# A decoder layer on one core: the input x also loaded transposed, small inputs joined, squares, angles and one score step moved

## The chip, the cores and the metric

The kernel runs on one core of a Trainium2 chip. The metric is the device time of one execution in microseconds (us). TensorE is called PE here, and its weight loads, which overlap the matmuls, PEld; VectorE is DVE, ScalarE is ACT, GpSimd is POOL, and SyncE, which issues most transfers, is SP. Each engine takes its own instructions strictly in the order of its queue, so that an instruction that waits holds up all behind it on that engine.

## What is computed

One layer over 256 tokens of 2048 channels: a root-mean-square norm, one wide projection, a recurrent branch and an attention branch with 32 query and 4 key heads, a gated merge, a second norm and an MLP. What matters here is the beginning:

```python
h = rmsnorm(x, norm_mix_pre[l])
proj = h @ w_in[l]
xr, yr, q, k, v, g_rnn, g_attn = jnp.split(proj, IN_OFFSETS, axis=-1)
...
q = rope(q.reshape(B, S, N_Q_HEADS, HEAD_DIM), positions)
k = rope(k.reshape(B, S, N_KV_HEADS, HEAD_DIM), positions)
```

The division by the norm is not applied to x before the projections. They run on x times the gain, and 1/rms of each token is multiplied in later, so the squares of x are needed only when the first results are used.

## The kernel before

**Two parts for each number.** Every matmul of the projections runs in a 32-bit format of reduced precision. Each operand is therefore split into a rounded high part and the rest, the low part, and a product is three matmuls: high by high, low by high, high by low. `Stream` does this for the weights. It loads them in halves of 128x1024 numbers (512 KB, tile `wraw`), ACT casts a half to the high part (`whi`, line 94), and DVE subtracts to get the low part (`wlo`, line 95). The halves 0 to 9 have buffers of their own; those behind share four (`WRAW`), so that the load of half j+4 waits for DVE's `wlo` of half j. The split parts have six buffers (`WHALF`), so that the cast of half j+6 waits until PE is through with half j. The splits run six halves ahead of PE (`AHEAD`).

**x.** PE needs x with channels on the partitions. Before, x arrives with tokens on the partitions, in two row blocks of four quarters (256 KB each, lines 336 and 339), PE transposes it in 32 blocks against an identity (`turn`, line 375, tile `ptr` in PSUM), ACT multiplies each block by the gain and casts it to the high part of `hT` (`part`, line 382), and DVE makes the low part (line 385). Both engines read PSUM there.

**The first projection.** `kv_step(j)`, for j from 0 to 7, multiplies two of the sixteen 128-channel blocks of x by half j of the key and value weights: 12 matmuls of 512 columns, into two banks `kv0` and `kv1` (line 396). Order in the code: the transposes of one quarter, its `part`, a split, a step, the next quarter's transposes. `pin` (keep_in_program_order) holds these instructions in the order in which the code is written; elsewhere a scheduler orders the instructions of each engine. In the last quarter `squares` sums the squares of x, four on ACT (line 405) and four on DVE (line 403).

**What follows.** For each of four groups of heads one pass over 8 halves for the gate (`g`) and one for the queries (`q`): 96 matmuls each (lines 294 to 298). Side work is written as generators in a list `waiting`; `pump()` runs the next piece, and is called after each half. The first is `keys_values`: it takes the norms (`first_norm`, with the square root on ACT), spreads 1/rms over the partitions with two small matmuls (`pr`, line 448, read from `spread`), scales the values, turns the keys by their angles (`rope`), and transposes them (`pk`, line 526). `attention(g)` follows; in it `scores` makes the products `sc` (line 560, pinned), and `masked` takes them out of PSUM on DVE (line 572). In the last group the third score step has to reuse the banks of the second, so that it waits for `masked` of the second.

The angles (position by frequency, reduced modulo two pi by nine small DVE instructions, then two sines on ACT) come behind the first projection, unpinned. Positions, frequencies, sinks and per-channel vectors are four small transfers on SP's queue, behind the first fourteen halves (lines 452 to 458).

Of the kernel before, what the change touches and what calls it, by code (L numbers as in the profile page):

```python
# [25 lines left out]
P = 128  # L26
# [27 lines left out]
class Stream:  # L54
# [3 lines left out]
    def __init__(self, nc, pool, chunks, room, sums):  # L58
        self.nc, self.pool, self.chunks, self.room, self.sums = nc, pool, chunks, room, sums
        self.raw, self.parts = {}, {}  # L60
        self.loaded = self.split = 0
        self.pin = lambda i: i
        self.high = []
        self.at = 0

# [101 lines left out]
def layer(tc, x, g_pre, pos_t, pos_row, inv_freq, vecs, sinks, gains, w_kv, w_q, w_xy, w_rg, w_g, w_rp, w_ap, w_out,  # L167
# [46 lines left out]
    def flat(t):  # L214
        return t.rearrange("p a b c -> p (a b c)")
# [111 lines left out]
    x_nat = [flat(unit(f"x{tb}", F32)) for tb in range(TB)]  # L327
# [4 lines left out]
    gcol = const.tile([P, KT], F32, name="gcol")  # L332
    nc.scalar.dma_start(gcol, g_pre)

    for q in range(4):
        nc.sync.dma_start(x_nat[0][:, quarter(q)], x_v[0][:, quarter(q)])
        if q == 0:
            ws.load_to(1)
        last = nc.sync.dma_start(x_nat[1][:, quarter(q)], x_v[1][:, quarter(q)])
        with tc.issue_after(last.ins):  # L340
            ws.load_to(2 * q + 2)
# [5 lines left out]
    st = const.tile([P, 32], F32, name="st")  # L347
    sq = const.tile([P, 4, TB, 4], F32, name="sqs")
# [20 lines left out]
    ps_t = {}  # L369

    def turn(tb, q):
        ps = ps_t[tb, q] = bank(psm, "ptr")
        for i in range(4):
            k = 4 * q + i
            pin(nc.tensor.transpose(ps[:, i * P : i * P + P], x_nat[tb][:, k * P : k * P + P], ident))

    def part(tb, q, ks=range(4)):
        t = slice(tb * P, tb * P + P)
        ps = ps_t[tb, q]
        for i in ks:  # L380
            g = gcol[:, 4 * q + i : 4 * q + i + 1]
            pin(nc.scalar.activation(hT[q][:, i, 0, t], ps[:, i * P : i * P + P], AF.Copy, scale=g))
        for i in ks:
            g = gcol[:, 4 * q + i : 4 * q + i + 1]
            pin(nc.vector.scalar_tensor_tensor(hT[q][:, i, 1, t], ps[:, i * P : i * P + P], g,
                                               hT[q][:, i, 0, t].bitcast(F32), ALU.mult, ALU.subtract))
# [3 lines left out]
    def kv_step(j):  # L390
        hi, lo = ws.half(False)
        for x, w in ((0, hi), (1, hi), (0, lo)):
            for tb in range(TB):
                for i in range(2):
                    kt = 2 * j + i
                    pin(mm(kv[tb], hT[kt // 4][:, kt % 4, x, tb * P : tb * P + P], w[:, quarter(i)],
                           start=kt == 0 and w is hi and x == 0, stop=kt == KT - 1 and w is lo))

    def squares(tb):
        for q in range(4):  # L400
            x, into = x_nat[tb][:, quarter(q)], sq[:, 0, tb, q : q + 1]
            if tb:
                pin(nc.vector.scalar_tensor_tensor(t2("j"), x, 1.0, x, ALU.mult, ALU.mult, accum_out=into))
            else:
                pin(nc.scalar.activation(t2("j"), x, AF.Square, accum_out=into))

    turn(0, 0)
    turn(1, 0)
    part(0, 0, (0, 1))
    ws.split_high()  # L410
    part(1, 0, (0, 1))
    ws.split_low()
    for tb in range(TB):
        part(tb, 0, (2, 3))
    ws.split_to(2)
    for q in range(4):
        kv_step(2 * q)
        if q < 3:
            turn(0, q + 1)
            turn(1, q + 1)  # L420
            part(0, q + 1)
            part(1, q + 1)
            ws.split_to(2 * q + 4)
        else:
# [9 lines left out]
    def first_norm():  # L434

        pr = bank(psm, "pr")
        spread = t2("spread")
        for tb in range(TB):
# [7 lines left out]
            dg = spread[:, tb * P : tb * P + P]  # L446
            nc.vector.tensor_scalar(dg, ident, r, None, ALU.mult)
            mm(pr[:, tb * P : tb * P + P], ones, dg, start=True, stop=True)
        nc.scalar.copy(rT, pr[:, 0:S])

    pos_i = pa.tile([P, TB], I32, name="pos_i")
    nc.sync.dma_start(pos_i, pos_t)
    ifr = pa.tile([P, 32], F32, name="ifr")
    nc.sync.dma_start(ifr, inv_freq.partition_broadcast(P))
    sink = pa.tile([P, NH], F32, name="sink")
    nc.sync.dma_start(sink, sinks.partition_broadcast(P))
    vec = pa.tile([P, 8, KT], F32, name="vec")
    nc.sync.dma_start(vec, vecs.rearrange("p (a b) -> p a b", a=8))

# [11 lines left out]
    def small(name, shape, dt=F32):  # L471
        return pa.tile(shape, dt, name=name)

    posf = small("posf", [P, TB])
    pin(nc.vector.tensor_copy(posf, pos_i))
    ang = small("ang", [P, TB, 32])
    for tb in range(TB):
        nc.vector.tensor_scalar(ang[:, tb, :], ifr, posf[:, tb : tb + 1], None, ALU.mult)
    turns = small("turns", [P, TB, 32])
    nc.vector.tensor_scalar(turns, ang, 1.0 / TWO_PI, None, ALU.mult)  # L480
    nc.vector.tensor_scalar(turns, turns, 12582912.0, 12582912.0, ALU.add, ALU.subtract)
    for part in two_pi_parts():
        nc.vector.scalar_tensor_tensor(ang, turns, -part, ang, ALU.mult, ALU.add)
    nc.vector.tensor_scalar(ang, ang, 3.1415925, -3.1415925, ALU.min, ALU.max)
    sn = turns
    nc.scalar.activation(sn, ang, AF.Sin)
    cc = small("cc", [P, TB, 2, 32])
    ss = small("ss", [P, TB, 2, 32])
    hs = small("hs", [P, TB, 32])
    nc.scalar.activation(hs, ang, AF.Sin, scale=0.5)  # L490
    nc.vector.tensor_tensor(hs, hs, hs, ALU.mult)
    for i in range(2):
        nc.vector.tensor_scalar(cc[:, :, i, :], hs, -2.0, 1.0, ALU.mult, ALU.add)
        nc.vector.tensor_scalar(ss[:, :, i, :], sn, 1.0 - 2.0 * i, None, ALU.mult)
# [20 lines left out]
    def keys_values(banks):  # L515
        yield
        first_norm()
        for tb in range(TB):
# [3 lines left out]
            rope(banks[tb][:, 0:256], tb, NKV, [k4[:, :, 0, :], k4[:, :, 1, :]])  # L522
            yield
            ps = bank(psm, "pk")
# [3 lines left out]
            yield  # L528

    yatt = []  # L530

    def attention(g, banks):
# [100 lines left out]
        masked(*two)  # L633
        if last_group:
            three = scores(1, 1, [bank(psb, "sc") for par in range(2)])
        yield
# [637 lines left out]
def lay_out(inp):  # L1274
# [26 lines left out]
    def down(w):  # L1301
# [6 lines left out]
    pos = np.asarray(inp["positions"]).reshape(TB, P)  # L1308
    return {
        "x": np.asarray(inp["x"]).reshape(S, D),  # L1310
        "g_pre": per_channel(g("norm_mix_pre")),
        "pos_t": pos.T,
        "pos_row": pos.reshape(S),
        "inv_freq": (10000.0 ** (-np.arange(0, HD, 2, dtype=np.float64) / HD)).astype(np.float32),
# [29 lines left out]
```

## Time and profile before

| What | Value |
|---|---|
| Median of three runs | 1512.02 us (1510.14, 1512.02, 1512.23) |
| The profiled execution | 1509.99 us |
| Its span, first to last instruction | 1508.2 us |
| PE busy | 1492.7 us (99%) |
| DVE busy | 1101.7 us (73%) |
| ACT busy | 828.7 us (55%) |
| Read from HBM | 288.60 MB, 196 GB/s over the span |
| First matmul of `kv_step` | 8.22 us after the span's start |
| First load of the gate pass `g` | 34.19 us |
| First load of the query pass `q` | 58.98 us |

How to read it: the span leaves out what lies before the first and behind the last instruction (1.8 us here). A row of the timeline gives start, duration, engine, line and operation, and in brackets the idle time before it with what ended it. A row of the waits gives the waiting engine, what it waited for, the total in us, the number of times and the longest. A row of the stages gives the stage, its length, the busy time of each engine with the number of instructions, the granted PE clock, and the share and rate of the transfers.

### The profile page before, as it was taken

What the parts mean: (1) busy time and instruction counts of PE and PEld (TensorE: products, weight loads), DVE (VectorE), ACT (ScalarE), POOL (GpSimd) and SP (SyncE); (2) the same over time, 40 slices, a digit from 0 to 9 for tenths busy, and PEclk for the clock granted to TensorE, in tenths of its full rate; (3) what the DMA queues carried; (4) which work ended last, traced back from release to release, by engine and by line L of the source; (5) the groups of instructions that cost most, each with busy time, mean ns of one, the idle gap of its engine ahead of it and who ended that gap; (6) DMA issues with size and microseconds to landing.
All of it is one profiled execution on the core that took longest, in us unless ns stands there. A gap on an engine that the chain in (4) does not pass through costs nothing.

```text
span 1508.2 us, 20012 instructions
## 1 busy us (share of the span) xinstructions
PE 1492.7 (99%) x7600; PEld 1261.5 (84%) x7600; DVE 1101.7 (73%) x1379; ACT 828.7 (55%) x1143; POOL 1.7 (0%) x9
## 2 busy tenths in 40 slices
PE   9999999999999999999999999999999999999997
PEld 7887787889888888888888888888888888888885
DVE  6675677858669966555667866698886666788897
ACT  6554665647566766443355655565454555555453
POOL 0000000000000000000000000000000000000000
PEclk9999999999999999999999999999999999999999
DMA  6645454465646566556764755566667565576665
GB/s 254 221 157 173 148 166 136 157 201 165 213 155 221 170 209 197 192 184 195 268 221 136 270 188 188 194 194 213 217 201 237 195 195 183 193 236 202 204 221 186
DMA packets 83327, 296.19 MB, mean 196 GB/s; under 512 B 9760, under 2 KB 10016, under 8 KB 82208
## 3 DMA queue, kind: packets, MB, share of 16 engines
q1 hardware_dynamic: 79920, 287.58, 57.6%
q10 hardware_dynamic: 3312, 7.35, 1.3%
q8 instruction: 59, 0.97, 0.3%
q14 instruction: 36, 0.29, 0.1%
HBM read 288.60 MB, written 6.29 MB: 196 GB/s over the span
## 4 chain that ended last, share of the span: by engine, by line
PE 84%; DVE 8%; DMA 4%; ACT 2%; issue 1%; DVEq 0%; SPq 0%; ACTq 0%
PE ps L256 21%; PE ps L254 11%; PE dQ L1111 5%; PE pp L298 4%; PE pp L294 4%; PE pp L296 4%; PE g L294 4%; DMA wraw<-in_w_dn 4%; PE g L298 4%; PE g L296 4%; DVE wlo L95 3%; PE s L1111 3%; PE dP L1111 2%; PE q L294 2%; PE q L298 2%; PE q L296 2%
## 5 line engine op out<-in xcount | busy, mean ns | idle before, releaser
L95 DVE TENSOR_TENSOR wlo<-wraw,whi 128x1024 fp32r<-128x1024 f32 x523 | 632.7, 1221 | 306.1 <-ACT whi L94 302.9
L94 ACT CAST whi<-wraw 128x1024 fp32r<-128x1024 f32 x523 | 544.2, 1052 | 554.0 <-PE ps L256 127.3
L256 PE MATMUL ps<-h2T,whi 128*128 128x512 f32 x960 | 223.9, 390 | 0.0
L256 PEld LDWEIGHTS ps<-h2T,whi 128*128 128x128 f32 x960 | 178.3, 188 | 35.6
L256 PE MATMUL ps<-hT,whi 128*128 128x512 f32 x512 | 121.3, 392 | 0.0
L254 PEld LDWEIGHTS ps<-h2T,wlo 128*128 128x128 f32 x960 | 119.1, 192 | 2.3
L254 PE MATMUL ps<-h2T,wlo 128*128 128x256 f32 x960 | 119.9, 283 | 0.0
L256 PEld LDWEIGHTS ps<-hT,whi 128*128 128x128 f32 x512 | 94.7, 188 | 19.8 <-issue 1.1
L1111 PE MATMUL dQ<-whi,uT 128*128 128x512 f32 x288 | 106.9, 389 | 0.0
L294 PE MATMUL g<-whi,hT 128*128 128x512 f32 x256 | 101.3, 396 | 0.0
L296 PE MATMUL g<-wlo,hT 128*128 128x512 f32 x256 | 100.1, 391 | 0.1
L298 PE MATMUL g<-whi,hT 128*128 128x512 f32 x256 | 99.9, 390 | 0.0
L254 PEld LDWEIGHTS ps<-hT,wlo 128*128 128x128 f32 x512 | 63.7, 192 | 1.8 <-issue 0.7
L254 PE MATMUL ps<-hT,wlo 128*128 128x256 f32 x512 | 64.7, 284 | 0.0
L1111 PEld LDWEIGHTS dQ<-whi,uT 128*128 128x128 f32 x288 | 54.1, 188 | 11.2
L294 PEld LDWEIGHTS g<-whi,hT 128*128 128x128 f32 x256 | 48.1, 188 | 10.5 <-issue 1.0
L296 PEld LDWEIGHTS g<-wlo,hT 128*128 128x128 f32 x256 | 48.1, 188 | 10.1 <-DVE wlo L95 0.5
L298 PEld LDWEIGHTS g<-whi,hT 128*128 128x128 f32 x256 | 48.1, 188 | 10.1
L1111 PE MATMUL dQ<-wlo,uT 128*128 128x512 f32 x144 | 56.1, 389 | 0.0
L1111 PE MATMUL dCs<-whi,uT 128*128 128x512 f32 x144 | 54.1, 389 | 0.0
L1111 PE MATMUL dP<-whi,uT 128*128 128x512 f32 x144 | 54.1, 389 | 0.0
L130 DVE TENSOR_TENSOR tlo<-t,thi 128x1536 fp32r<-128x1536 f32 x28 | 49.2, 1757 | 5.1 <-ACT thi L129 5.1
(285 smaller groups left out, 2461.6 us busy)
## 6 DMA issues: line engine op xcount, KB each, us to landing
wraw<-in_w_up SPq DMA_DIRECT2D x128, 512.0 KB, 3.9
wraw<-in_w_dn SPq DMA_DIRECT2D x128, 512.0 KB, 4.5
wraw<-in_w_g SPq DMA_DIRECT2D x64, 512.0 KB, 4.7
wraw<-in_w_xy SPq DMA_DIRECT2D x64, 512.0 KB, 3.7
wraw<-in_w_q SPq DMA_DIRECT2D x32, 512.0 KB, 4.3
wraw<-in_w_ap SPq DMA_DIRECT2D x32, 512.0 KB, 4.8
wraw<-in_w_rp SPq DMA_DIRECT2D x32, 512.0 KB, 4.6
wraw<-in_w_out SPq DMA_DIRECT2D x32, 512.0 KB, 4.9
```

Source lines behind the costliest of these rows:

```text
L94: self.pin(self.nc.scalar.copy(hi, src))
L95: self.pin(self.nc.vector.tensor_tensor(lo, src, hi.bitcast(F32), ALU.subtract))
L130: v.tensor_tensor(lo, t, hi.bitcast(F32), ALU.subtract)
L254: mm(ps[:, f, 1, :], w, a[:, 0, :], start=False, stop=j == 1 and k == 7)
L256: mm(ps[:, f].rearrange("p a b -> p (a b)"), w, a.rearrange("p a b -> p (a b)"), start=kt == 0, stop=j == 3 and k == 7)
L294: mm(banks[tb][n], a[:, 0, t], hi[:, n * 512 : n * 512 + 512], start=first, stop=False)
L296: mm(banks[tb][n], a[:, 0, t], lo[:, n * 512 : n * 512 + 512], start=False, stop=False)
L298: mm(banks[tb][n], a[:, 1, t], hi[:, n * 512 : n * 512 + 512], start=False, stop=last)
L1111: mm(b, a[x], w[y], start=not begun and i == 0, stop=tail and i == 2)
```

## The change

**x comes twice.** The host lays x out a second time with channels on the partitions (`x_t`). Four transfers of 512 KB, the first cut in two, bring it, interleaved with the weight halves, which now come first. `part(k)` takes a whole 128x256 block from SBUF, once on ACT and once on DVE: 16 instructions each where 32 stood. The transposes `turn` are gone. x in its old layout is still loaded for the squares, in eight quarters, behind weight half 11.

**The first half** is split in two pieces of 512 columns (`split_first`), with a `part` between each cast and its subtraction, and step 0 runs one block of channels after the other.

**Small inputs.** Gain, frequencies, sinks, eight vectors and positions come in one transfer of 128x210 numbers (`few`, 105 KB) on ACT's queue at the start. ACT loads its function table before the first data are there (a copy of `eps`).

**Moved.** The angles are a generator of which a piece runs after each of steps 4 to 7, the sines stand behind step 7, pinned before the rest; all eight squares are on ACT and two pieces of `keys_values`; the two matmuls `pr` come last in `keys_values`. In the last group of `attention` the third score step is written one piece later.

```diff
+    def split_first(self, between):
+        src = self.raw.pop(0)
...
+        for i in range(2):
+            c = slice(i * 512, i * 512 + 512)
+            self.pin(self.nc.scalar.copy(hi[:, c], src[:, c]))
+            between(i)
+            self.pin(self.nc.vector.tensor_tensor(lo[:, c], src[:, c], hi[:, c].bitcast(F32), ALU.subtract))
...
-    for q in range(4):
-        nc.sync.dma_start(x_nat[0][:, quarter(q)], x_v[0][:, quarter(q)])
-        if q == 0:
-            ws.load_to(1)
-        last = nc.sync.dma_start(x_nat[1][:, quarter(q)], x_v[1][:, quarter(q)])
-        with tc.issue_after(last.ins):
-            ws.load_to(2 * q + 2)
+    tiny = const.tile([P, 210], F32, name="tiny")
+    nc.scalar.dma_start(tiny, few)
...
+    ws.load_to(1)
+    load_xt(0, 2)
+    load_xt(2, 4)
+    ws.load_to(2)
+    for q in range(1, 4):
+        load_xt(4 * q, 4 * q + 4)
+        ws.load_to(2 * q + 2)
+    ws.load_to(12)
+    x_nat = [[t2("xq") for q in range(4)] for tb in range(TB)]
+    for tb in range(TB):
+        for q in range(4):
+            nc.sync.dma_start(x_nat[tb][q], x_v[tb][:, quarter(q)])
     ws.load_to(2 * EXTRA + WRAW)
...
+    nc.scalar.activation(st[:, 30:31], eps, AF.Copy)
...
+    def part(k):
+        q, i, g, src = k // 4, k % 4, gcol[:, k : k + 1], xt(k)
+        pin(nc.scalar.activation(hT[q][:, i, 0, :], src, AF.Copy, scale=g))
+        pin(nc.vector.scalar_tensor_tensor(hT[q][:, i, 1, :], src, g, hT[q][:, i, 0, :].bitcast(F32), ALU.mult,
+                                           ALU.subtract))
...
-    for q in range(4):
-        kv_step(2 * q)
-        if q < 3:
-            turn(0, q + 1)
-            turn(1, q + 1)
-            part(0, q + 1)
-            part(1, q + 1)
-            ws.split_to(2 * q + 4)
-        else:
-            ws.pin = lambda i: i
-            squares(0)
-            squares(1)
-            ws.split_to(2 * q + 4)
-        kv_step(2 * q + 1)
+    ws.split_first(part)
+    kv_step(0)
+    angle = angles()
+    for j in range(1, 8):
+        for i in range(2):
+            part(2 * j + i)
+        ws.split_high()
+        ws.split_low()
+        kv_step(j)
+        if j > 3:
+            next(angle, None)
+    sines()
+    ws.pin = lambda i: i
     ws.ahead(ws.at - 1)
...
     def keys_values(banks):
         yield
-        first_norm()
+        squares(0)
+        yield
+        squares(1)
+        yield
+        spread = first_norm()
...
+        spread_r0(spread)
...
         masked(*two)
+        yield
         if last_group:
             three = scores(1, 1, [bank(psb, "sc") for par in range(2)])
-        yield
+            yield
         masked(*three)
```

**How the order moves, first place: PE between step 0 and step 2 of the first projection.** `kv0` and `kv1` are the two result banks, `whi1` and `wlo1` the split parts of weight half 1, `ptr` the transposes. Before:

```order
L396 MATMUL kv1_138<-wlo0_159,hT0_133 128x512 x2
L375 MATMUL ptr_185<-ident_111,x0_76 128x128 x4
L375 MATMUL ptr_190<-ident_111,x1_77 128x128 x4
L396 MATMUL kv0_137<-whi1_169,hT0_133 128x512 x2
L396 MATMUL kv1_138<-whi1_169,hT0_133 128x512 x2
L396 MATMUL kv0_137<-wlo1_170,hT0_133 128x512 x2
L396 MATMUL kv1_138<-wlo1_170,hT0_133 128x512 x2
```

Now:

```order
L415 MATMUL kv1_152<-wlo0_160,hT0_147 128x512
L415 MATMUL kv0_151<-whi1_185,hT0_147 128x512 x2
L415 MATMUL kv1_152<-whi1_185,hT0_147 128x512 x2
L415 MATMUL kv0_151<-wlo1_187,hT0_147 128x512 x2
L415 MATMUL kv1_152<-wlo1_187,hT0_147 128x512 x2
L415 MATMUL kv0_151<-whi2_205,hT1_148 128x512 x2
```

The block of eight transposes between the steps is gone, here and at two more places, and the eight ahead of step 0.

**Second place: ACT behind the cast of weight half 10**, which belongs to the gate pass. `xq` are the quarters of x, `turns` and `hs` the two sines, `v_sb` the scaled values. Before:

```order
L94 CAST whi10_395<-wraw10_103 128x1024
L94 CAST whi11_399<-wraw11_105 128x1024
L94 CAST whi12_403<-wraw12_107 128x1024
L94 CAST whi13_460<-wraw13_109 128x1024
L94 CAST whi14_478<-wraw14_407 128x1024
L358 ACT_TABLE_LOAD
L358 ACTIVATE st_114<-st_114,eps_112 128x1 x2
```

Now:

```order
L107 CAST whi10_349<-wraw10_100 128x1024
L421 ACTIVATE xq_104,sqs_129<-xq_104 128x512
L421 ACTIVATE xq_105,sqs_129<-xq_105 128x512
L421 ACTIVATE xq_106,sqs_129<-xq_106 128x512
L107 CAST whi11_353<-wraw11_102 128x1024
L421 ACTIVATE xq_107,sqs_129<-xq_107 128x512
L421 ACTIVATE xq_108,sqs_129<-xq_108 128x512
L450 ACT_TABLE_LOAD
L450 ACTIVATE turns_155<-ang_154 128x64
L451 ACTIVATE hs_158<-ang_154 128x64
L107 CAST whi12_357<-wraw12_120 128x1024
L421 ACTIVATE xq_109,sqs_129<-xq_109 128x512
```

Two more squares, the cast of half 13 and the table load for the square root follow. So all eight squares, a table load and the two sines now stand between the casts of the halves 10 and 13, which stood side by side. On DVE the product of `hs` now stands ahead of `wlo11`.

**Third place: PE at the third score step of the last group**, in the first product of the recurrent branch (`ps`); `sc` are the scores. Before:

```order
L254 MATMUL ps_2332<-hT2_135,wlo77_2166 128x256 x4
L254 MATMUL ps_2332<-hT3_136,wlo77_2166 128x256 x2
L560 MATMUL sc_2359<-kT_457,qT3_2187 128x256
L254 MATMUL ps_2332<-hT3_136,wlo77_2166 128x256
L560 MATMUL sc_2360<-kT_457,qT3_2187 128x256
L254 MATMUL ps_2332<-hT0_133,wlo78_2205 128x256 x4
```

Now:

```order
L267 MATMUL ps_2260<-hT2_149,wlo77_2094 128x256 x4
L267 MATMUL ps_2260<-hT3_150,wlo77_2094 128x256 x2
L579 MATMUL sc_2302<-kT_377,qT3_2115 128x256
L267 MATMUL ps_2260<-hT3_150,wlo77_2094 128x256
L579 MATMUL sc_2303<-kT_377,qT3_2115 128x256
L267 MATMUL ps_2260<-hT0_147,wlo78_2133 128x256 x4
```

The scheduler puts the third score step at the same place among the matmuls as before, although the code has it one piece later.

More of the change, by code (lines that the diff above doesn't have):

```diff
@@ L391, in kv_step @@
         hi, lo = ws.half(False)
[L392 to L397, printed above, removed]
+        for ks in ((0,), (1,)) if j == 0 else ((0, 1),):
+            for x, w in ((0, hi), (1, hi), (0, lo)):
+                for tb in range(TB):
+                    for i in ks:
+                        kt = 2 * j + i
+                        pin(mm(kv[tb], hT[kt // 4][:, kt % 4, x, tb * P : tb * P + P], w[:, quarter(i)],
+                               start=kt == 0 and w is hi and x == 0, stop=kt == KT - 1 and w is lo))
```

136 lines of the change are left out of this document (62 added, 74 removed).

## The prediction

> **What bounds the kernel now.** First the page: its span, its busy times and the chain of work that ended last.
>
> ```profile
> span 1508.2 us, 20012 instructions
> PE 1492.7 (99%) x7600; PEld 1261.5 (84%) x7600; DVE 1101.7 (73%) x1379; ACT 828.7 (55%) x1143; POOL 1.7 (0%) x9
> PE 84%; DVE 8%; DMA 4%; ACT 2%; issue 1%; DVEq 0%; SPq 0%; ACTq 0%
> ```
>
> PE sets the end: 99% busy, 84% of the chain. So the change is worth what it takes out of PE's queue: matmuls that vanish, waits that vanish, and an earlier first matmul; busy time saved on ACT and DVE counts only where PE waited for it. Next the stages of the beginning: up to the first load of the gate pass, that pass, and the first query pass.
>
> ```profile
> 0.00:34.19 34.19, 31.77 (x148) 25.60 (x149) 20.94 (x51) 22.17 (x52) 1.70 (x9) 1.00 0.75 280
> 34.19:58.98 24.79, 23.91 (x110) 19.08 (x109) 21.82 (x55) 17.32 (x23) 0.00 (x0) 1.00 0.60 210
> 58.98:80.75 21.77, 21.77 (x98) 18.04 (x97) 9.80 (x9) 10.03 (x11) 0.00 (x0) 1.00 0.59 192
> ```
>
> The query pass shows the floor: 96 matmuls in 21.77 us, 0.2268 us each, and nothing else. The gate pass has the same 96 and takes 24.79 us. The first projection has 96 too, and ends only at 34.19. Where the difference lies, PE's first row there, the chain and PE's waits tell:
>
> ```profile
> 8.22 2.13 PE L396 MATMUL kv<-whi,hT 128*128 128x512 f32 x8
> ```
>
> ```profile
> 1.64 5.82 DMA x<-in_x
> 11.85 0.87 PE ptr L375 x8
> 18.53 0.87 PE ptr L375 x8
> 25.20 0.87 PE ptr L375 x8
> ```
>
> ```profile
> PEld kv L396 <- ACT whi L94: 1.3, 3, 0.4
> PE kv L396 <- DVE wlo L111: 0.3, 1, 0.3
> PEld pr L448 <- DVE spread L447: 1.2, 1, 1.2
> PEld g L296 <- DVE wlo L95: 0.5, 1, 0.5
> PEld pk L526 <- DVE k L509: 0.3, 1, 0.3
> ```
>
> From the first projection matmul at 8.22 to 34.19 are 25.97 us. They are 96 × 0.2268 = 21.77, three blocks of eight transposes 2.6, three waits for a cast 1.3 and one for DVE 0.3: in sum 26.0. The gate pass loses 0.5 to a late `wlo`, 1.2 to the norm's `spread` and 0.3 to the keys.
>
> **The change part by part.** *Transposes and the first projection.* With the transposes gone a step needs its weight half, two blocks of x, ACT and DVE. The rows for their prices:
>
> ```profile
> 5.64 0.33 SPq L339 DMA_DIRECT2D x<-in_x  x1
> 8.74 0.33 SPq L76 DMA_DIRECT2D wraw<-in_w_kv  x1
> 20.48 0.33 SPq L454 DMA_DIRECT2D ifr<-in_inv_freq  x1
> 10.00:15.00 5.00, 4.69 (x25) 3.69 (x24) 4.27 (x12) 3.74 (x11) 0.00 (x0) 1.00 1.03 407
> 20.00:25.00 5.00, 4.99 (x22) 3.76 (x21) 4.43 (x10) 3.06 (x7) 0.00 (x0) 1.00 1.02 405
> L94 ACT CAST whi<-wraw x7: 1042/1102/1108, 10.0 to 28.6; 128x1024 fp32r<-128x1024 f32 x7
> L722 ACT ACTIVATE xct<-px,vec x16: 587/590/606, 255.9 to 523.4; 128x256 f32<-128x256 f32 x16
> L725 DVE SCALAR_TENSOR_TENSOR xct<-px,vec,xct x48: 472/477/486, 258.2 to 525.6; 128x255 f32<-128x255 f32 x16, 128x254 f32<-128x254 f32 x16, 128x253 f32<-128x253 f32 x16
> 33.64 5.76 DVE L95 TENSOR_TENSOR wlo<-wraw,whi 128x1024 fp32r<-128x1024 f32 x5
> ```
>
> An issue on SP waits until the transfer eight places ahead of it has landed. So the first three rows are landings: weight half 0 by 5.64, half 1 at 8.74, half 7 at 20.48. The windows show that transfers then run at 405 to 407 GB/s, 1.29 us for 512 KB. In the new order exactly as many bytes lie ahead of the end of half 1 (two halves and 512 KB of x), and of half 7, plus the 105 KB of small inputs, 0.27 us. So half 1 lands at 9.0 and half 7 at 20.75.
>
> Per step of two blocks ACT needs 2 × 0.59 for the blocks, no row having this operation itself and L722 being the nearest (same size, also from SBUF), plus 1.04 for the cast: 2.2 us. DVE needs 2 × 0.48 and 1.15 (five `wlo` in 5.76): 2.1; the spread angles add at most four small instructions in a step, when DVE is ahead of PE by more than that. PE needs 12 × 0.2268 = 2.72, the transfers 768 KB, 1.94. PE is the slowest again, once it runs.
>
> What starts it: half 0 and the first blocks have 768 KB ahead of them, as half 0 had, so 5.64 + 0.27 = 5.9; the block's 0.59 on ACT gives the first matmul at 6.6 (8.22 before). Step 0's twelve end at 9.3, some 9.6 with its waits for DVE. That is off the path, for step 1 must have half 1: 9.0, a cast of 1.04 and 0.1 of semaphores, so 10.15. From there seven steps of 2.72 follow; half 2 lands at 11.6, is cast by 12.7, and PE comes to it at 12.9, the closest; half 7 is there 5 us early. The gate pass starts at 10.15 + 19.05 = 29.2: **5.0 us** saved.
>
> *The gate pass.* Casts of its halves no longer wait behind the transposes' work, so the 0.5 goes. `pr` moves into the query pass. Left are 96 matmuls and eight transposes:
>
> ```profile
> 54.22 0.54 PE pk L526 x4
> 57.09 0.44 PE pk L526 x4
> 44.62 0.49 PE pr L448 x2
> ```
>
> 21.77 + 2 × 0.45 = 22.7 for 24.79: **2.1 us** saved; `pr` costs its **0.5** in the query pass, where it needs a bank that ACT's copy of the first keys frees; that copy stands behind the cast of half 20, near 51 by the same reckoning as below, and PE comes at 54.7.
>
> *The second copy of x and the squares.* 2.1 MB more to load, eight squares on ACT instead of four, and the sines, all ahead of casts that the gate pass needs. I cost it at nothing; the cover is this:
>
> ```profile
> 30.20 0.68 ACT L405 ACTIVATE j<-x 128x512 f32<-128x512 f32 x1
> 30.81 0.67 ACT L405 ACTIVATE j<-x 128x512 f32<-128x512 f32 x1
> L358 ACT ACT_TABLE_LOAD  x1: 1283/1283/1283, 42.2 to 42.2; - x1
> ```
>
> Squares come 0.62 apart. Quarters three and five of x land at 20.75 + four halves + three or five times 0.65: 27.9 and 29.1. ACT: third square to 28.5, cast of half 11 to 29.5, two squares to 30.7, table 1.28 to 32.0, sines 0.4. DVE: `hs` and four small ones to 33.1, then `wlo11` to 34.2. PE needs it at 29.2 + 3 × 2.72 + 0.2 = 37.6: 3.4 us to spare, the thinnest place. Half 13 is cast by 36.3, and its `wlo` is there at 37.5 for 42.9. The load of half 15 waits for `wlo11`, and lands near 39 for 48.3. The keys leave the banks by 44.5; the query pass takes them at 51.9.
>
> *The last scores.* PE's wait there, and what DVE does:
>
> ```profile
> 262.61 0.29 PEld L560 LDWEIGHTS sc<-kT,qT 64*128 64x128 f32 x2 [1.33 <-DVE s L572]
> 261.88 1.28 DVE L572 SCALAR_TENSOR_TENSOR s<-sc,mask 128x512 f32<-128x512 f32 x2
> ```
>
> The programs stand in the same order here, on PE and, up to this `masked`, on DVE. A wait between the same instructions at the same distances stays: **0**. Bounds: 1.33 gained if the DVE backlog thins out, and, for the pieces behind it that do move, 0.8 lost, twice the wait of this row:
>
> ```profile
> PEld pt L618 <- DVE s L601: 0.4, 1, 0.4
> ```
>
> *The early table load*, by this row:
>
> ```profile
> ACT L382 <- DMA gcol<-in_g_pre: 4.6, 1, 4.6
> ```
>
> ACT waited for the gain and loaded its table behind that, yet the transposes that it then needed ended later still: 0. The sum: 5.0 + 2.1 − 0.5 = **6.6 us**. Everything behind is the same program 6.6 us earlier.
>
> **The rivals.** *The last scores' wait goes too.* For it: that is what the edit is written for. Against: the unchanged order. Gain 6.6 + 1.3 = 7.9.
>
> *The first step runs at half pace.* The same transposes before and after:
>
> ```profile
> 1.08 4.34 PEld L366 LDWEIGHTS warm<-ones 128*128 128x128 f32 x20 [1.08 <-DVE ones L350]
> 5.30 0.87 PEld L375 LDWEIGHTS ptr<-ident,x 128*128 128x128 f32 x4
> 7.50 0.42 PEld L375 LDWEIGHTS ptr<-ident,x 128*128 128x128 f32 x4 [1.33 <-DMA x<-in_x]
> ```
>
> Four took 0.87 at 5.30 and 0.42 at 7.50, and the warm-up had the slow pace too, though the windows' granted clock is 1.00 throughout. The change leaves PE idle from 5.4 to 6.6, and then starts. Should the slow pace last over step 0, its twelve take 5.4 us, to 12.0 instead of 10.15: gain 4.7. Against it: the change of pace came by 7.5 although PE had idled for 1.3. The Trainium skill (TensorE: Matmul & The Clock Gate, What's actually happening) says that PE runs at half its clock until it has been busy for a free-running window of about 3.4 us. By that rule, and as an estimate, a missed window costs up to 1.7 us; the two rows agree with it in the pace, and no row here shows where the windows lie.
>
> *Slower: the fifth quarter of x holds up `wlo11`.* The place is ACT's queue: sines behind the fifth square, `hs` ahead of `wlo11`, and PE behind that. It decides once that quarter lands 3.4 + 1.0 us late (its square waited 1.0 for ACT), at 33.5; each us beyond is a us of PE. To eat 6.6 it must land after 40, so that 3.4 MB behind half 7 take 19 us: 176 GB/s where the windows show 405. Landing at 42: 1512 against 1510, slower. A milder case, 37 to 40, leaves a gain of 0 to 3.
>
> **How the numbers follow.** The profiled execution took 1509.99 us, span 1508.2 and 1.8 around it; minus 6.6 is 1503.4. The median of the runs shown is 2.0 higher, at 1512.02, the lowest 1510.14, so 1503.5 to 1505.6 by the runs. I take 1505, near the median.
>
> Chances: forecast 0.63; scores too 0.10 (1503.7); half pace 0.17 (1506.9); x late, but still a gain of under 3 us, 0.07 (1510); x so late that it is slower 0.03. A measurement here tells about 0.2%, 3 us, from no change: faster by more 0.90, within 0.07, slower 0.03. The range: low end a gain of 7.9 and half 1 landing 0.6 earlier than reckoned, from the lowest base, 1501.5; high end a gain of 4.7 less the 0.8 of the pieces that move, from the median, 1508. The rest outside is 0.1 and the runs' own spread.
>
> **What would show it.** Right: no `ptr` of `in_x`; first projection matmul near 6.6, one wait of PE for the cast of half 1 that ends near 10.2, no wait of steps 2 to 7; first gate load at 29 to 30, first query load near 52; `pr` without a wait; `sc` still waiting 1.3 for DVE. Wrong: PE waiting for `wlo11` to `wlo14` or for `pk`, transfers under 350 GB/s between 20 and 32 us, a first step of over 4 us, or the 6.6 us reached at the query pass and lost again behind it, which only the moved pieces of the last group could do.

## The result, and the profile after

| | Before | After |
|---|---|---|
| Median of five runs, us | 1511.99 (1509.31 to 1512.23) | 1504.83 (1504.39 to 1506.64) |
| Ratio, with its 95% interval | 1 | 0.9960 (0.9945 to 0.9974) |
| Profiled execution, us | 1509.99 | 1504.41 |
| Its span, us | 1508.2 | 1502.6 |

The change takes 0.4% off. First the page of the changed kernel: span, busy times, and the chain of work that ended last.

```profile
span 1502.6 us, 19925 instructions
PE 1487.6 (99%) x7568; PEld 1259.3 (84%) x7568; DVE 1096.6 (73%) x1356; ACT 829.9 (55%) x1137; POOL 1.7 (0%) x9
PE 97%; DVE 2%; ACT 1%; DMA 0%; issue 0%; DVEq 0%; SPq 0%; ACTq 0%
```

The first and third line are worth a second look beside those of before. The chain was PE for 84% before, with 12% of DVE and transfers; it is PE for 97% now. So in the execution before, another chain than PE's set the end: from 1320 us on it has no row of PE. That is taken up below.

The stages of the beginning, in the same columns as before (up to the gate pass, the gate pass, the first query pass):

```profile
0.00:30.80 30.80, 27.70 (x116) 22.98 (x117) 21.46 (x43) 23.34 (x42) 1.71 (x9) 0.94 0.96 364
30.80:53.58 22.78, 22.78 (x106) 18.88 (x105) 16.98 (x39) 17.05 (x26) 0.00 (x0) 1.00 0.69 229
53.58:75.72 22.14, 22.14 (x103) 18.39 (x102) 9.79 (x9) 10.21 (x12) 0.00 (x0) 1.00 0.61 206
```

The gate pass has fallen from 24.79 to 22.78, which is 2.0, and PE waits for nothing in it; the query pass has grown from 21.77 by 0.37. But the gate pass starts at 30.80, not at 29.2: the first projection saved 3.4 us where 5.0 were forecast. The number behind the clock's column of the first row says why, 0.94. Finer stretches of the same kernel, with the granted clock as the third number from the end:

```profile
8.22:8.32 0.10, 0.10 (x2) 0.01 (x1) 0.10 (x1) 0.10 (x2) 0.00 (x0) 0.97 0.80 328
8.32:8.42 0.10, 0.10 (x2) 0.00 (x0) 0.10 (x2) 0.10 (x1) 0.00 (x0) 0.50 1.31 533
11.63:11.73 0.10, 0.10 (x2) 0.04 (x1) 0.10 (x2) 0.10 (x1) 0.00 (x0) 0.51 1.02 410
11.73:11.83 0.10, 0.10 (x2) 0.10 (x1) 0.10 (x2) 0.10 (x1) 0.00 (x0) 1.00 0.90 369
```

PE ran at half its clock from 8.32 to 11.73, 3.41 us, right behind its first matmul. That matmul was late too. The row of its weight load in the timeline, and then the piece of the chain in order of time that stands ahead of it (start and length):

```profile
7.41 0.30 PEld L415 LDWEIGHTS kv<-whi,hT 128*128 128x128 f32 x2 [2.21 <-ACT hT L402]
```

```profile
1.18 5.58 DMA xt<-in_x_t
```

The matmul came at 7.41, because the first blocks of x landed at 1.18 + 5.58 = 6.76; PE had been idle for 2.2 us when it started. Last, the wait of the third score step, and the last instructions of PE and of DVE:

```profile
257.63 0.29 PEld L579 LDWEIGHTS sc<-kT,qT 64*128 64x128 f32 x2 [1.33 <-DVE s L591]
...
1492.60 0.39 PE L1131 MATMUL dQ<-whi,uT 128*128 128x512 f32 x1
...
1498.02 0.75 DVE L1280 SCALAR_TENSOR_TENSOR x<-t,st,x 128x512 f32<-128x512 f32 x1
```

The scores wait 1.33 us, as before. PE ends at 1492.99 and DVE at 1498.77. The distance between these two ends is called the lag from here on: 5.78 us.

### The profile page after: what moved, and what is told of

It reads as the page before. It is cut to its first block, busy times and chain, and to the rows that moved or that the text cites. A ratio compares the mean times of both kernels' runs of the same rounds, so it can differ in the third digit from the quotient of the medians.

```text
span 1502.6 us, 19925 instructions
## 1 busy us (share of the span) xinstructions
PE 1487.6 (99%) x7568; PEld 1259.3 (84%) x7568; DVE 1096.6 (73%) x1356; ACT 829.9 (55%) x1137; POOL 1.7 (0%) x9
## 3 DMA queue, kind: packets, MB, share of 16 engines
HBM read 290.69 MB, written 6.29 MB: 198 GB/s over the span
## 4 chain that ended last, share of the span: by engine, by line
PE 97%; DVE 2%; ACT 1%; DMA 0%; issue 0%; DVEq 0%; SPq 0%; ACTq 0%
PE ps L269 22%; PE ps L267 12%; PE dQ L1131 9%; PE s L1131 5%; PE dP L1131 4%; PE g L307 4%; PE g L309 4%; PE g L311 4%; PE pp L309 4%; PE pp L307 4%; PE pp L311 4%; PE dCs L1131 3%; PE q L307 2%; PE q L311 2%; PE q L309 2%; PE o L311 2%
## 5 line engine op out<-in xcount | busy, mean ns | idle before, releaser
L108 DVE TENSOR_TENSOR wlo<-wraw,whi 128x1024 fp32r<-128x1024 f32 x516 | 624.2, 1220 | 312.1 <-ACT whi L107 309.5
L107 ACT CAST whi<-wraw 128x1024 fp32r<-128x1024 f32 x516 | 537.9, 1051 | 546.6 <-PE ps L269 132.1
```

The source lines that it names most:

```text
L107: self.pin(self.nc.scalar.copy(hi, src))
L108: self.pin(self.nc.vector.tensor_tensor(lo, src, hi.bitcast(F32), ALU.subtract))
```

## The experiments

Six numbers of each profiled execution carry what follows: the start of the gate pass, the length of that pass, the stretch from the second group's gate pass to the first product `pp` (in it lie the last scores), the end of the last matmul, the lag, and the span. The time is 1.8 us longer than the span.

| Kernel | Gate from | Gate pass | Second gate pass to `pp` | Last matmul ends | Lag | Span |
|---|---|---|---|---|---|---|
| before | 34.19 | 24.79 | 217.52 | 1498.19 | 6.22 | 1508.20 |
| after | 30.80 | 22.78 | 217.35 | 1492.99 | 5.78 | 1502.62 |
| after, the repeat | 29.45 | 22.78 | 217.35 | 1491.64 | 6.95 | 1502.46 |
| 16 warm-up matmuls | 29.85 | 22.81 | 218.93 | 1493.60 | 6.13 | 1503.61 |
| 1 warm-up matmul | 31.55 | 22.78 | 217.40 | 1493.77 | 7.41 | 1505.04 |
| scores back | 31.82 | 22.81 | 217.59 | 1494.29 | 5.77 | 1503.92 |
| scores later | 29.28 | 22.79 | 216.97 | 1491.89 | 6.88 | 1502.65 |
| no second copy of x | 29.25 | 22.80 | 218.74 | 1492.95 | 7.60 | 1504.38 |
| before, fewer transposes | 30.66 | 24.76 | 219.02 | 1496.01 | 6.38 | 1506.18 |
| late second copy of x | 30.44 | 30.45 | 218.90 | 1501.84 | 6.51 | 1512.61 |
| GpSimd | 28.88 | 22.80 | 218.91 | 1497.48 | 7.88 | 1509.24 |
| GpSimd, 16 warm-up | 29.34 | 22.78 | 217.39 | 1496.44 | 7.89 | 1508.18 |
| 16 warm-up, 4 additions fewer | 29.44 | 22.81 | 217.39 | 1491.88 | 5.78 | 1501.55 |

The theory at the start: transposes and waits removed from PE's queue are the gain, and the half clock took 1.4 us of it.

**More and less warm-up.** Edit of the changed kernel:

```diff
-WARM = 10
+WARM = 16
```

> The changed kernel with 16 instead of 10 warm-up matmuls, so that TensorE is busy until about the first projection matmul at 7.4. Theory (the idle 2.0 us between warm-up and first matmul lose the full pace, which then costs 1.4 us): granted clock 1.00 in every half us from 7.5 to 12.5, first matmul at 7.4 to 8.0, first gate load at 29.3 to 29.9 against 30.80, profiled time 0.9 to 1.5 under the changed kernel's 1504.4. Rival (the dip from 8.2 to 11.7 has nothing to do with the gap): clock 0.50 there again, gate at 30.8 to 31.4, time the same or 0.6 longer. Second rival (half 1 of the weights sets step 1 anyway): clock 1.00, but the gate still at 30.8.

Measured: clock 1.00 from 7.5 to 12.5, first matmul at 7.96, gate pass from 29.85. The first rival is out, the second too. Yet the median is 1505.17 (1503.63 to 1506.19), not lower, and the profiled execution took 1505.39, 1 us more than the changed kernel's in spite of the earlier gate. So something behind gave the gain back. Part of it is in the table's third column, 1.6 us too long. The windows there:

```profile
255.60:259.02 3.42, 2.29 (x11) 1.45 (x12) 3.42 (x7) 2.93 (x10) 0.00 (x0) 1.00 0.47 133
259.02:262.43 3.41, 3.41 (x18) 3.41 (x18) 3.41 (x5) 0.00 (x0) 0.00 (x0) 0.50 0.34 110
262.43:265.85 3.42, 3.42 (x17) 2.79 (x16) 1.86 (x4) 1.05 (x1) 0.00 (x0) 1.00 0.66 217
```

Again 3.41 us at half the clock, right behind the wait of the last scores. The other direction:

```diff
-WARM = 10
+WARM = 1
```

> The changed kernel with one warm-up matmul instead of ten. Theory (the pace depends on how busy TensorE has been in the last few us): half pace from the first projection matmul at 7.4 on for 3.4 us or more, step 0's twelve take 4.5 to 5.4 us, first gate load at 31.2 to 32.7, 0.4 to 1.9 later than 30.80. Rival (a dip at a fixed time after the start): gate at 30.8, dip again from 8.2 to 11.7.

Measured: gate from 31.55, half pace throughout step 0 and into step 1, as the theory had it; median 1506.80, ratio 0.9969 (0.9957 to 0.9981).

**The changed kernel once more, the repeat.** No edit.

> The changed kernel itself once more. Theory (the clock is granted by windows of 3.41 us that run free of the program): another start of the windows, so step 0 and step 1 run at half pace for another stretch, the gate starts anywhere from 29.4 to 32.5 instead of 30.80, and the gate and query pass take 22.8 and 22.1 again. Rival (the dip belongs to the program): half pace from 8.3 to 11.7 again and the gate at 30.8 within 0.2.

Measured: gate from 29.45. Four matmuls of step 0, the same in each kernel: the changed kernel, its repeat, and the kernel of the next paragraph, which has the same beginning, each in its own view of the timeline.

```profile
9.55 1.91 PE L415 MATMUL kv<-whi,hT 128*128 128x512 f32 x4
```

```profile
9.26 1.08 PE L415 MATMUL kv<-whi,hT 128*128 128x512 f32 x4
```

```profile
10.07 1.91 PE L415 MATMUL kv<-whi,hT 128*128 128x512 f32 x4
```

One beginning, three fates: slow, fast, slow. In 3.41 us of step 1, PE issued 16 recorded matmuls in the repeat and 9 in the kernel of the next paragraph (the repeat first):

```profile
9.69:13.10 3.41, 3.41 (x16) 2.82 (x15) 3.34 (x6) 3.09 (x6) 0.00 (x0) 1.00 1.02 410
```

```profile
9.88:13.29 3.41, 3.41 (x9) 2.63 (x9) 3.31 (x5) 3.04 (x7) 0.00 (x0) 1.00 1.00 410
```

The clock's column reads 1.00 in both, so in the first microseconds, before the first change that is on record, it does not tell the pace; the instructions do. The clock changes at the ends of windows of 3.41 us whose phase differs from one execution to the next (8.32 and 11.73 in the changed kernel's profile, 6.28 in the repeat's record of the clock). The Trainium skill (TensorE: Matmul & The Clock Gate, What's actually happening) describes just this, a window of 3413 ns that runs free of the kernel; the runs agree with it in the length and in the free phase. From the first matmul to the gate it takes 21.89 us in the repeat, with the scores later and with GpSimd, 23.39 in the changed kernel's profile and 24.48 with the scores back; the first matmul itself comes between 6.99 and 7.56 in these five. So the gate starts anywhere from 28.9 to 31.8 in kernels with one and the same beginning. The forecast's 29.2 is reached within 0.3 where the clock holds.

But this execution's span is 1502.46, against 1502.62, though its last matmul ended 1.35 us earlier. The lag took it: 6.95 instead of 5.78.

**The last scores as they were, and really later.**

```diff
         masked(*two)
-        yield
         if last_group:
             three = scores(1, 1, [bank(psb, "sc") for par in range(2)])
-            yield
+        yield
```

> The changed kernel with the last group's third score step written where it was before. Theory: TensorE comes to it at the same place, its wait for DVE is 1.3 again, and the stretch from the last group's first gate load to the first pp product stays 56.8 within 0.2; the pieces behind it go back one place, which moves at most 0.4. Rival (the edit gave the 0.4 that the end of the program gained): the time from the last group to the end is 0.4 longer. Rival (it costs): 0.4 to 0.8 shorter.

Measured: 217.59 for 217.35, so the edit is worth 0.24 us in these two executions, through the pieces behind the scores (a wait of 0.4 us of `pt` for DVE is back, which the kernel before has too), and the step's own wait is unmoved. The end's rivals are out: from `pp` to the end 1209.57 against 1209.55.

```diff
         masked(*two)
         yield
         if last_group:
+            yield
+            yield
             three = scores(1, 1, [bank(psb, "sc") for par in range(2)])
```

> The changed kernel with the last group's third score step written two pieces later still, so that it does move among TensorE's matmuls, by 31 rows of the recurrent branch. Theory (the edit as made left TensorE's order and so the wait alone): the 1.3 us wait of the scores for DVE goes, and the stretch from the first load of the second gate pass to the first pp product is 217.35 - 1.3 = 216.0, if the transposes of the shares (pt) behind it do not come to wait. Rival (the chain of exponents behind the scores is as tight, so the wait goes over to pt): 217.0 to 218.5.

Measured: the scores' wait is gone, and 216.97 is only 0.38 less. Three other waits of PE in that stretch tell where the 1.33 went (columns: duration of the wait in brackets, with its releaser):

```profile
279.62 0.64 PEld L637 LDWEIGHTS pt<-ident,s 128*128 128x128 f32 x6 [0.95 <-DVE s L620]
...
281.81 0.90 PEld L637 LDWEIGHTS pt<-ident,s 128*128 128x128 f32 x8 [0.82 <-ACT pT L639]
...
291.18 0.19 PEld L307 LDWEIGHTS pp<-whi,yatt 128*128 128x128 f32 x1 [0.81 <-DVE py L757]
```

The rival was right but for 0.03 us: the exponents behind the scores are as tight, and the wait goes over to `pt` and to the first `pp`. These are idle times of weight loads, which PE bridges in part, so they do not add up to the change of the stretch. Behind `pp` PE lost another 0.8 us in this execution (1200.71 us to the last matmul, 1199.92 in the changed kernel); why stays open.

**Transposes alone.** In the kernel before, the transposes of the quarters 1 to 3 are left out:

```diff
-            turn(0, q + 1)
-            turn(1, q + 1)
+            ps_t[0, q + 1], ps_t[1, q + 1] = ps_t[0, 0], ps_t[1, 0]
```

> The kernel before with the 24 later transposes of x left out (the quarters 1 to 3 of hT are made from quarter 0's transposes, so three quarters of x are left out of the result). Theory (the transposes and the waits for casts behind them are the loss): first matmul at 8.2 as before, first gate load 3.9 earlier, 30.3 instead of 34.19. Rival (only the transposes' own 2.6 us go, the casts stay late since ACT still reads 32 small blocks): 31.6. Rival (the transfers bound the steps): later than 32.5.

Measured: gate from 30.66, 3.53 us earlier. Of this, 0.22 lie ahead of the first matmul (8.00 for 8.22), which the edit does not touch. The transposes' own time was 2.6, so some 0.7 us of the waits behind them went along. Of the 4.74 that the change saves up to the gate at full clock, these 3.31 are seven tenths; the rest is an earlier first matmul (7.56 for 8.22, 0.66) and other waits (0.77).

**The second copy of x.** First without it:

```diff
-            nc.sync.dma_start(x_nat[tb][q], x_v[tb][:, quarter(q)])
...
-            x, into = x_nat[tb][q], sq[:, 0, tb, q : q + 1]
+            x, into = xt(8 * tb + 2 * q, 2), sq[:, 0, tb, q : q + 1]
```

> The changed kernel without the second copy of x: the squares are taken from the transposed x, over the wrong axis, so the norms are left out of the result; ACT does the same work. Theory (the second copy is hidden): gate pass 22.8 and query pass 22.1 as before, the gate pass's start only moved by the clock's windows (29.9 to 32), all other stretches within 0.2. Rival (2.1 MB more ahead of halves 12 to 19 cost something in the query pass or later): up to 1 us shorter there.

Measured: gate pass 22.80, query pass 22.14: the copy costs nothing in these passes. The 1.4 us more at the last scores are again a stretch at half clock there. Then the same copy late. One kernel loaded transposed x again ahead of it:

```diff
+    for i in range(8):
+        nc.sync.dma_start(xts[0][:, 0 : 4 * S], x_t[i % 4])
     x_nat = [[t2("xq") for q in range(4)] for tb in range(TB)]
```

> The changed kernel with 4 MB of idle transfers (transposed x loaded again into a tile that is done with) ahead of the second copy of x. Theory (the fifth quarter holds up the sines, hs and with them wlo11, and TensorE loses each us by which that quarter lands after about 34.6): it lands near 39.5, TensorE waits about 4 to 6 us in the gate pass for wlo11 and wlo12, gate pass 27 to 29 us instead of 22.8. Rival (only the norm needs x, at 44 and later): the gate pass is 23 to 24, with a wait at the first pk.

It says nothing on the question: these loads stand ahead of the first use of that tile, so the first projection itself waited for them, to 54.4 us. Another loads the second copy itself three times over:

```diff
+    for again in range(3):
         for tb in range(TB):
             for q in range(4):
                 nc.sync.dma_start(x_nat[tb][q], x_v[tb][:, quarter(q)])
```

> The changed kernel with the second copy of x loaded three times over (the same numbers into the same tiles), so that its fifth quarter lands some 10 us later than at 29.2, at 39 to 40, or later still where a load waits for the one before. Theory (the fifth quarter holds up the sines, hs and with them wlo11; TensorE loses each us by which it lands after the gate's start + 3.8): gate pass 22.8 plus 4 to 7 us, the wait put down to wlo of halves 11 and 12. Rival (only the norm needs x): gate pass 22.8 to 24, with a wait at pk.

Measured: gate pass 30.45, the time 1514.39 in the one execution, above every run of the kernel before (1513.72 at most). What PE waited for in the pass, then ACT's first square in the timeline, then two stretches of the pass:

```profile
PEld g L307 <- ACT whi L107: 4.4, 1, 4.4
PEld g L309 <- DVE wlo L108: 1.0, 1, 1.0
```

```profile
37.95 0.63 ACT L422 ACTIVATE xq<-xq 128x512 f32<-128x512 f32 x1 [8.89 <-DMA xq<-in_x]
```

```profile
41.73:45.15 3.42, 0.00 (x0) 0.00 (x0) 0.99 (x6) 3.41 (x9) 0.00 (x0) 1.00 1.02 400
45.15:51.98 6.83, 5.83 (x13) 4.27 (x14) 6.32 (x13) 4.84 (x8) 0.00 (x0) 0.50 0.68 226
```

The slower rival exists, but not by the link that was named: the scheduler put the sines ahead of the squares here, and it was the squares themselves that kept ACT from casting half 11. The waits are 5.4 us; the pass grew by 7.7, since the idle window cost two windows at half clock behind it.

**The end.** The lag was 5.8 to 7.6 us in the kernels above the last three rows of the table, and in each with a lag over 6 the page's chain leaves PE for DVE and transfers, as it did before (in one with 5.77 it does so too, for a part). This is the repeat's:

```profile
PE 85%; DVE 7%; DMA 4%; ACT 2%; issue 1%; DVEq 0%; ACTq 0%
```

New theory: in the last product, DVE's queue behind the transfers of the last weights is a second bound. DVE splits these weights, each load waits for a buffer that DVE frees, and DVE has the last additions to do. Two rows of the repeat's chain show the link: the load starts as DVE's subtraction ends.

```profile
1471.03 1.23 DVE wlo L108
1472.27 5.57 DMA wraw<-in_w_dn
```

DVE's waits from 1340 to 1500, changed kernel first, repeat below (total, times, longest):

```profile
DVE t L136 <- DMA wraw<-in_w_dn: 3.7, 6, 1.1
...
DVE acc L1266 <- PE dCs L1131: 1.3, 1, 1.3
```

```profile
DVE t L136 <- DMA wraw<-in_w_dn: 5.4, 6, 1.4
...
DVE t L136 <- PE dCs L1131: 0.3, 1, 0.3
```

In the first, DVE is through with its backlog and waits for PE's last results; in the second it waits longer for transfers, and PE's last results wait for it.

The forecast below adds that this bound eats what PE gains beyond about 5.2 us. The traces do not show that, since the stretch that it bounds starts with the last product, earlier when PE comes to it earlier. From that product's first matmul (at 1333.19 before, 1328.07 in the changed kernel, 1326.72 in the repeat) to DVE's end it is 171.23, 170.69 and 171.87 us, and 170.7 to 172.7 in the kernels above the last three rows of the table, without a clear order by the start. So as far as the traces show, the lag is drawn in each execution, and the 6.22 of the kernel before lies among the draws; whether an earlier PE makes long lags more frequent stays open.

Two ways to relieve DVE. The first moves twelve instructions to the idle GpSimd:

```diff
-                nc.vector.tensor_tensor(acc[tb][:, c], acc[tb][:, c], g3[:, c], ALU.mult)
+                nc.gpsimd.tensor_tensor(acc[tb][:, c], acc[tb][:, c], g3[:, c], ALU.mult)
...
-                nc.vector.tensor_tensor(t, t, acc[tb][:, quarter(2 * n + i)], ALU.add)
+                nc.gpsimd.tensor_tensor(t, t, acc[tb][:, quarter(2 * n + i)], ALU.add)
```

> The changed kernel with twelve 128x512 element-wise instructions of the last stage on GpSimd instead of VectorE (the additions of the sums kept away, L1240, and the multiplications by the gain, L1255, 0.68 us each on VectorE). Theory (the end has a second bound: VectorE's queue behind the transfers of the last weights, which eats what TensorE gains beyond about 5.2 us; the lag between the last matmul's end and VectorE's last instruction is 5.8 us where TensorE alone sets it, and was 5.8 to 7.6 in the runs so far): the lag is 5.8 to 5.9, the median 0.3 to 1.2 below the changed kernel's 1504.8. Rival (the lag comes with the output's transfers): lag 6 to 7.6 as before, time the same. Rival (GpSimd is slow and holds up VectorE): lag over 7.6, time over 1505.5.

Measured: 1511.41, ratio 1.0003 (0.9994 to 1.0012): all of the gain is gone. The same with 16 warm-up matmuls:

> The same with 16 warm-up matmuls. Theory (both bounds moved): clock 1.00 from 8 us on, gate at 29.3 to 29.9, lag 5.8 to 5.9, median 1503.0 to 1503.8, 1.0 to 1.8 below the changed kernel's 1504.8; more where the scores' wait for VectorE lets the clock fall at 255 to 262. Rival (the warm-up brings nothing, as its median of 1505.17 suggests): 1504.5 to 1505.2.

Measured: 1509.96, ratio 0.9995 (0.9986 to 1.0004); gate from 29.34 as expected, lag 7.89. Of the 6.6 us that the first GpSimd kernel's span is longer than the changed kernel's, 4.5 lie ahead of the last matmul's end and 2.1 in the lag. From `pp` to the last matmul PE takes 1204.76 and 1204.79 us in these two kernels, 1199.92 in the changed one. Two rows of the waits of the first of them, from 1300 on, tell of both:

```profile
PEld dQ L1131 <- DVE wlo L108: 2.1, 2, 1.8
DVE acc L1266 <- POOL t L1240: 2.0, 2, 1.2
```

The groups of instructions from 1400 to 1490 of the changed kernel, then of the first GpSimd kernel (busy us, mean ns), and GpSimd's own group from 1200 on:

```profile
L108 DVE TENSOR_TENSOR wlo<-wraw,whi 128x1024 fp32r<-128x1024 f32 x32 | 38.5, 1220 | 4.3 <-ACT whi L107 4.2
...
L139 DVE TENSOR_TENSOR t<-wraw 128x512 f32<-128x512 f32 x7 | 4.8, 687 | 0.1
```

```profile
L108 DVE TENSOR_TENSOR wlo<-wraw,whi 128x1024 fp32r<-128x1024 f32 x32 | 41.5, 1326 | 8.9 <-ACT whi L107 8.9
...
L139 DVE TENSOR_TENSOR t<-wraw 128x512 f32<-128x512 f32 x7 | 5.9, 847 | 0.2
```

```profile
L1240 POOL TENSOR_TENSOR t<-t,acc 128x512 f32<-128x512 f32 x8 | 12.0, 1526 | 1458.3 <-DVE t L1173 1452.3 <-DVE t L1175 6.0
```

GpSimd needs 1.53 us where DVE needs 0.68, and DVE's own instructions get longer beside it. This `wlo`, which ran while GpSimd was at work, took 2.32 us where the mean was 1.22:

```profile
1401.24 2.32 DVE L108 TENSOR_TENSOR wlo<-wraw,whi 128x1024 fp32r<-128x1024 f32 x1
```

The second rival was right. The scheduler also placed other work of DVE in the last product differently here, and in the first of the two kernels the clock fell once more, at 1418, so the loss is not GpSimd's alone; how it divides was not tried. The Trainium skill (GPSIMD Engine Reference, Specifications) says that GpSimd shares its interfaces to SBUF with VectorE, with contention for instructions of two SBUF inputs; the lengthened rows agree. So a cleaner relief: 16 warm-up matmuls, and only the last pass's four additions left out, with every other instruction in its place.

```diff
         def early(ready):
             for (tb, i), t in ready.items():
-                nc.vector.tensor_tensor(t, t, acc[tb][:, quarter(2 * n + i)], ALU.add)
+                if n == 0:
+                    nc.vector.tensor_tensor(t, t, acc[tb][:, quarter(2 * n + i)], ALU.add)
```

> The changed kernel with 16 warm-up matmuls and without the last four additions of the sums kept away (L1240 in the last pass, 2.7 us of VectorE in all; that part of the sum is left out of the result); the order of all other instructions is that of the kernel with 16 warm-up matmuls, 1505.17 us median. Theory (VectorE's queue behind the transfers of the last weights is a second bound of the end): the lag between the last matmul's end and VectorE's last instruction falls to 5.8 to 5.9, the span ends 9.6 after the last matmul, and the median is 1503.3 to 1504.6, 0.6 to 1.9 lower. Rival (VectorE's backlog is not what holds the end, only the transfers or the clock): lag 6.1 to 7.6 as in the other runs, median 1505.0 to 1505.4.

Measured: median 1503.36 (1502.72 to 1504.47), ratio 0.9944 (0.9931 to 0.9958), against 1505.17 with the additions. The last instructions, DVE's wait for PE, and the page's chain:

```profile
1491.49 0.39 PE L1131 MATMUL dQ<-whi,uT 128*128 128x512 f32 x1
...
1496.91 0.75 DVE L1281 SCALAR_TENSOR_TENSOR x<-t,st,x 128x512 f32<-128x512 f32 x1
```

```profile
DVE acc L1267 <- PE dCs L1131: 0.4, 1, 0.4
```

```profile
PE 97%; DVE 2%; ACT 1%; DMA 0%; issue 0%; DVEq 0%; ACTq 0%
```

The lag is 5.78, the chain is PE's again, and the earlier gate arrives at the end. With PE ending at 1491.88 the span is 1501.55; the repeat, with PE's end at 1491.64, had 1502.46. The forecast held, and its rival did not. Yet that taking 2.7 us of work off DVE shortens the lag is supported and not shown: it is one profile, the changed kernel and the one with the scores back have the same lag of 5.78 and 5.77 with all additions, and the two ratios, 0.9944 (0.9931 to 0.9958) and 0.9956 (0.9943 to 0.9970) without the edit, have intervals that overlap. Of the 1.8 us between the medians some may be other draws of the clock behind the last scores. What the traces do show is the second bound itself, in the executions whose chain leaves PE. This kernel leaves work out, so it is no better version; of those that leave nothing out, none was measurably faster than the changed kernel.

## Why the prediction was right, point by point

The time was forecast well, in part by luck. The sum from the profiled execution gave 1503.4; the two profiles took 1504.41 and 1504.24, for reasons that the sum did not have. The 1.6 us that were added for the base cover them, though they were not meant for that.

**Sum of PE's savings: right.** 6.6 us were forecast. In the repeat, where the clock held, the last matmul ended 1498.19 − 1491.64 = 6.55 us earlier: 4.74 up to the gate (forecast 5.0), 2.01 in the gate pass (2.1), −0.37 for `pr` (−0.5), 0.17 in the last group.

**Start of the first projection.** "Half 1 lands at 9.0" and sets step 1 at 10.15: at full clock it was the first matmul that set it, at 7.0 to 8.0 instead of 6.6. The first loads landed later than the 5.9 that was reckoned, and a cast was left out: ACT takes the first piece of half 0 (0.62 us) ahead of the block. The repeat's chain up to the first matmul:

```profile
0.74 5.55 DMA wraw<-in_w_kv
6.31 0.62 ACT whi L73
7.00 0.52 ACT hT L402
```

In it the weights came last, at 6.29; in the first profile it was the blocks of x, at 6.76. Step 1's first weight load then starts at 10.41 instead of 10.15, without a wait for the cast of half 1. This is the 0.26 missing from the 5.0.

**The half-pace rival.** It was put down as a rival with 0.17 and a gain of 4.7. It came true in the profiled execution, at 3.4 instead of 5.0 for this stage, and was absent in others; it is a draw in each execution and not one answer. The rows that were set against it, a change of pace in spite of 1.3 us of idleness, came from one execution, and so from one draw of the window's phase.

**"Everything behind is the same program 6.6 us earlier": the step that did not hold.** PE's last matmul is not the end. Behind it stands DVE's lag, 5.78 us where PE sets it and up to 7.6 where the last weights do. The first page's chain, PE 84%, DVE 8%, DMA 4%, held this already: it was read as PE being the bound, with the rest as trimmings, while those 12% were one piece, the last part of the program. In the repeat 6.55 us of PE's time became 5.7 of span; in the first profile 5.20 became 5.6, since its lag was 0.4 shorter than the one before.

**The base.** 1505 was taken since the runs' median was 2.0 above the profiled execution. From median to median the change took 7.2 us off, more than the 6.55 that PE saves at full clock; the spread of the runs, 2 to 3 us on each side, covers the difference. Of the two profiled executions of the changed kernel one lost 1.4 to the clock and nothing to the lag, the other nothing to the clock and 1.2 to the lag. The executions of the kernel before can draw the same losses; only one of them is profiled, so it is argued and not shown that this is why their median lies 2 us above that one.

**No cost for the second copy, the squares, the sines: right**, and the cover is real: PE waited nowhere in the gate pass, and lost 5.4 us of waits once the copy landed some 11 us later. **Last scores 0: right** at the wait, 0.2 off for the pieces behind. **The price of `pr`:** 0.37 for 0.5, without a wait.

## What to carry to other kernels

- An engine busy for 99% need not set the end: read from which time on the chain of waits leaves it for good, here 1320 of 1508 us. A saving ahead of that place moves all behind it; but the length of what is behind was drawn anew in each execution, over 2 us, so that 6.6 us at PE's last matmul came out as 5.6 and 5.7 in two pairs of profiles.
- To judge a change of a few us in 1500, compare stages and ends of engines in two profiles, and profile one kernel twice: two executions of one program differed by 1.35 us at PE's last matmul and by 0.16 at the end.
- Work moved to an idle engine must be priced on the engines beside it too.

## What the hardware showed that was not expected

- Half clock comes in whole windows of 3.41 us and depends on how busy PE was in the window ahead. In the changed kernel PE was busy for 1.40 of the 3.42 us before the drop at 8.32:

```profile
4.90:8.32 3.42, 1.40 (x8) 0.89 (x7) 0.93 (x2) 2.09 (x5) 0.00 (x0) 1.00 1.01 393
```

In the kernel before with fewer transposes, whose windows lie alike (laid back by whole windows from a change at 260.90), it was busy for 1.64, and the clock held. So a window need not be idle throughout to lose the clock.
- Behind the last scores the clock fell in six of the thirteen profiles in which they waited, for 1.4 to 1.6 us each time, though PE was busy for 2.3 to 2.4 of 3.4 us in the window before it, far more than the 1.64 that held at the start, and in others it held at 2.3. By the weight loads (the column behind PE's) the two kinds part better: 1.23 to 1.60 us in the six that fell, 1.60 to 2.10 in the seven that held. What the clock goes by stays open.
- A wait can cost more than itself: 5.4 us of waits for the late x made the pass 7.7 us longer.
